# A Mamba-2 mixer on one core: x turned by VectorE through DRAM instead of by TensorE

## The chip, the core and the metric

The kernel runs on one core of one Trainium2 chip. The core has TensorE (PE in the profile; PEld is its weight load), VectorE (DVE), ScalarE (ACT), GpSimd (POOL) and SyncE (SP, which issues nearly all DMAs here). Each engine runs its own instructions in order and waits on semaphores for the others. The metric is the device time of the whole program in microseconds (us).

## The reference

A trunk of two layers on x of 2048 tokens by 1024 features, fp32. Layer 0 runs RG-LRU heads and latent attention side by side; layer 1 is a Mamba-2 mixer (SSD) with four groups. The change is in layer 1 alone:

```
proj = x @ w_in                                  # z 2048, xbc 3072, dt 32
xbc  = silu(conv4(xbc));  x, B, C = split(xbc)   # causal depthwise convolution, 4 taps
xf   = x * dt;  cs = cumsum(dt * a) over 128 tokens
decay[l,s] = exp(cs[l] - cs[s]) for s <= l
y    = (C B^T * decay) xf + exp(cs) * (C state)
state = state * exp(cs[-1]) + B^T (xf * exp(cs[-1] - cs))
y    = rmsnorm_per_group((y + d * x) * silu(z)) @ w_out
```

## The kernel before

Layer 1's projection and scan are one phase, `phase_ssd`, between some 1170 and 2350 us of the span. It has 16 **stages** n, four groups of heads g with four pieces c of 512 tokens in each. A stage computes ten projection **units** of 128 by 512: z0 to z3 (numbers 0 to 3), B (4), C (5) and x0 to x3 (6 to 9). Two units are worked as a pair. Full precision comes from three matmuls of high and low halves, so a pair takes 48 matmuls in four **ticks** of twelve; a stage has 20 ticks. The order of the units is the list that `unit_order` gives.

Everything else is laid between the matmuls by hand: `self.later(k, fn)` puts the instructions of `fn` into the program k ticks later. So the order on each engine is the order of the program, and nothing is rearranged at run time. After an x, B or C unit `conv` follows: ScalarE reads the unit out of PSUM (L1130), VectorE adds the three other taps (L1136), ScalarE applies SiLU (L1138).

While a stage projects, the four **steps** of the stage before are run, one for each 128 tokens, five ticks apart. A step has these parts, at ticks counted from its own start:

- `prep` at -4: SP loads the decays' tile e, 512 KB, from d_cs (L1216; L1124 loads a small table, `tab`, for j = 0). e has two buffers.
- `expo` at -1: ScalarE turns e into decays (L1223, L1224).
- `turn` at 0: x stands with features on partitions, and the scan wants tokens there. TensorE transposes the four 128x128 blocks into one PSUM bank px (L1231), transposes B (L1233) and forms C times B (L1234).
- `spread` at 0: VectorE reads px three times (L1242 t1, L1249 xf, L1256 xs), masks C B (L1246) and multiplies e by it (L1250).
- `split` at +2 (xd), `products` at +4 (TensorE L1273: e times xf; the old state) and `products2` with `state` at +5.
- `norm` at +6: ScalarE squares y and sums the squares (L1309). It needs some tile to write the squares to, and takes the first half of e.
- `scale` at +8, `back` at +10: VectorE turns y in 32x32 blocks into yo (L1319).
- `write` at +12: four SP stores of yo, 64 KB each, in pieces of 128 bytes, to d_y1 (L1325; the profile names it d_y).

The projected x1T is read through a ring of ten blocks of 512 KB (L1103): two loads in the middle of a stage, six in its last pair, each as a block comes free. Between two groups ten blocks of weights are loaded (L98) and split (L112, L129) by `load_at`, into slots that the units have finished with. After the last stage come four more steps, four ticks apart, and the output projection (L1401 to L1418), whose weights `out1_weights` loads over the last stage. A DMA on SP also has to wait until the eighth DMA before it has landed.

Of the kernel before, what the change touches and what calls it, by code (L numbers as in the profile page):

```python
# [14 lines left out]
P = 128  # L15
# [42 lines left out]
class K:  # L58
# [96 lines left out]
    def run(self):  # L155
        nc, tc, A = self.nc, self.tc, self.A
        with ExitStack() as ctx:
            dp = ctx.enter_context(tc.tile_pool(name="dram", bufs=1, space=bass.MemoryType.DRAM))
            core = ctx.enter_context(tc.tile_pool(name="core", bufs=1))
            ctx.enter_context(tc.manual_schedule())  # L160
            self.W = core.tile([P, 10, 2048], F32R, name="W")
            self.core = core
            self.stp = ctx.enter_context(tc.tile_pool(name="stp", bufs=2))
            self.ring = core.tile([P, 10, 1024], F32R, name="ring")
            self.cst = core.tile([P, NCST], F32, name="cst")
            self.im = core.tile([P, 2, 128], F32R, name="im")
            self.half = core.tile([P, 2], F32, name="half")
            nc.vector.memset(self.half[:, 0:1], -0.5)
            nc.vector.memset(self.half[:, 1:2], 0.5)
            self.ident = self.cst[:, C_ID:C_ID + 128]  # L170
            D = self.D = {}
            D["y0"] = dp.tile([NT, P, KB, P], F32, name="d_y0")
            D["sg"] = dp.tile([4, P, SEQ], F32, name="d_sg")
            D["kr"] = dp.tile([NCH, P, 2, 512], F32R, name="d_kr")
            D["q"] = dp.tile([8, NCH, P, 512], F32, name="d_q")
            D["k"] = dp.tile([4, NCH, P, 2, 512], F32R, name="d_k")
            D["x1"] = dp.tile([SEQ, DM], F32, name="d_x1")
            D["x1T"] = dp.tile([NCH, P, KB, 2, 512], F32R, name="d_x1T")
            D["li"] = dp.tile([len(GROUPS), 512], F32, name="d_li")
            D["cs"] = dp.tile([NT, 32, P], F32, name="d_cs")  # L180
            D["tab"] = dp.tile([NCH, 4, P, 4, 5, 8], F32, name="d_tab")

            D["y1"] = dp.tile([NT, 32, 4, 16, P], F32, name="d_y1")
            self.pp = ctx.enter_context(tc.tile_pool(name="ps", bufs=8, space=bass.MemoryType.PSUM))
            self.layer0()
            with ExitStack() as c2:
                self.l1c = c2.enter_context(tc.tile_pool(name="l1c", bufs=1))
                self.xst = self.l1c.tile([P, 2, 512], F32, name="xst")
                self.o0 = ExitStack()
                self.phase_out0(self.o0.enter_context(tc.tile_pool(name="o0", bufs=2)))  # L190
                with ExitStack() as c3:
                    self.phase_ssd(c3)
                    self.flush_of("phase_ssd")
            self.phase_out1()
            self.dump()
# [910 lines left out]
    def phase_ssd(self, ctx):  # L1106
# [16 lines left out]
            t = S[n]["tab"] = p.tile([P, 4, 5, 8], F32, tag="tab", name="tab", bufs=2)  # L1123
            nc.sync.dma_start(out=t, in_=D["tab"][c, g])  # L1124

        def conv(g, u, ps, o):

            b = blk(g, 6 + u if u < 4 else u)
            w = lambda k: vec[:, b, k:k + 1]
            nc.scalar.activation(out=o, in_=ps, func=AF.Identity, scale=w(3), bias=w(4))  # L1130

            def taps():
                for k in range(3):
                    d = 3 - k
                    for dst, src in ((o[:, d:], ps[:, :512 - d]), (o[:, :d], halo[:, u, k:])):
                        v.scalar_tensor_tensor(out=dst, in0=src, scalar=w(k), in1=dst, op0=ALU.mult, op1=ALU.add)  # L1136
                v.tensor_copy(halo[:, u], ps[:, 509:512])
                self.later(1, lambda: nc.scalar.activation(out=o, in_=o, func=AF.Silu))  # L1138
            self.later(1, taps)

        def terms(n, s):
            for kb in range(KB):
# [7 lines left out]
        def post(n, s, ps):  # L1150
            g, c = divmod(n, NCH)
            st = S[n]
            if s < 4:
                z = st["z", s] = p.tile([P, 512], F32, tag="z", name="z", bufs=6)
                nc.scalar.activation(out=z, in_=ps, func=AF.Silu)
            elif s >= 6:
                o = st["x", s - 6] = pc.tile([P, 512], F32, tag="xT", name="xT", bufs=7)
                conv(g, s - 6, ps, o)
            else:
                nm = "BC"[s - 4]  # L1160
                o = st[nm] = pc.tile([P, 512], F32, tag=nm, name=nm, bufs=2)
                conv(g, s, ps, o)
# [39 lines left out]
        def step(n, j, t0):  # L1202
# [16 lines left out]
            def expo():  # L1219
# [3 lines left out]
                    nc.scalar.activation(out=e[:, hd], in_=e[:, hd], func=AF.Relu, scale=-1.0, bias=cs[:, hd:hd + 1])  # L1223
                nc.scalar.activation(out=e, in_=e, func=AF.Exp, scale=-1.0)  # L1224

            def turn():

                st = S[n]
                px = R["px"] = self.psum()
                for u in range(4):  # L1230
                    nc.tensor.transpose(px[:, u * 128:u * 128 + 128], st["x", u][:, tok], self.ident)  # L1231
                pb = R["pb"] = self.psum()
                nc.tensor.transpose(pb[:, 0:128], st["B"][:, tok], self.ident)  # L1233
                nc.tensor.matmul(pb[:, 128:256], st["B"][:, tok], st["C"][:, tok], start=True, stop=True)  # L1234

            def spread():
                dt, cs, ecs, dd, cd = R["t"]
                px, pb = R["px"], R["pb"]
                xs = R["xs"] = p.tile([P, 512], F32, tag="xs", name="xs")
                if not last:  # L1240
                    t1 = R["t1"] = p.tile([P, 512], F32, tag="t1", name="t1")
# [63 lines left out]
            def norm():  # L1305
                y = R["y"]
                q = R["q"] = p.tile([P, 4], F32, tag="q", name="q", bufs=2)
                j2 = R["e"][:, 0:4].rearrange("p k n -> p (k n)")
                nc.scalar.activation(out=j2, in_=y, func=AF.Square, accum_out=q[:, 0:1])  # L1309
                nc.gpsimd.tensor_scalar(out=q[:, 1:2], in0=q[:, 0:1], scalar1=1.0 / 512, scalar2=1e-6, op0=ALU.mult, op1=ALU.add)  # L1310
                nc.gpsimd.tensor_tensor(out=q[:, 2:3], in0=q[:, 1:2], in1=self.half[:, 0:1], op=ALU.pow)

# [2 lines left out]

            def back():

                o = R["o"] = p.tile([P, 512], F32, tag="yo", name="yo", bufs=2)
                v.transpose(out=o, in_=R["y"])  # L1319

            def write():
                o = R["o"]
# [1 line left out]
                    r = slice(32 * b, 32 * b + 32)  # L1324
                    nc.sync.dma_start(out=D["y1"][tt, :, g, :, r], in_=o[r].rearrange("r (u s) -> r u s", s=32))  # L1325

            for at, fn in ((-4, prep), (-1, expo), (0, turn), (0, spread), (2, split), (4, products), (4, out), (5, products2), (5, state),
                           (6, norm), (8, scale), (10, back), (12, write)):
                self.later(t0 + at, fn)

# [9 lines left out]
        def unit_order(n):  # L1340
            if n == 0:
                return [4, 5, 6, 7, 8, 9, 0, 1, 2, 3]
            if n == N - 1:
                return [0, 1, 6, 7, 2, 8, 3, 4, 9, 5]
            return [4, 5, 6, 7, 8, 0, 1, 2, 3, 9] if n % NCH == 0 else [4, 5, 0, 6, 1, 7, 2, 8, 3, 9]

        for n in range(N):
            g, c = divmod(n, NCH)
# [2 lines left out]
                for j in range(4):  # L1351
                    step(n - 1, j, 5 + 5 * j)
            if c == NCH - 1 and g + 1 < 4:
                for s, at in ((4, 1), (5, 2), (6, 6), (7, 10), (8, 14), (0, 16), (1, 19), (2, 21), (3, 24), (9, 26)):
                    self.load_at(at, self.wslot(s), A["w1"][g + 1, s])
            if n == N - 1:
                self.out1_weights()
# [20 lines left out]
    def out1_weights(self):  # L1378
# [1 line left out]
        self.o1w = {}  # L1380
        self.nw = self.core.tile([P, 16], F32, name="nw")
        self.nc.sync.dma_start(out=self.nw, in_=self.A["nw"])
        for k, (sl, at) in enumerate(((4, 5), (5, 8), (6, 9), (0, 12), (1, 13), (2, 15), (3, 16), (8, 18), (9, 19), (7, 21))):
            self.o1w[k] = self.W[:, sl]
            self.load_at(at, sl, self.A["wo1"][k], rows=self.nw[:, 2 * (k % 8):2 * (k % 8) + 2])

# [226 lines left out]
```

## Time and profile before

| | us |
|---|---|
| median of 3 runs | 2650.51 (2649.64 to 2654.17) |
| profiled execution, whole | 2655.34 |
| its span, first to last instruction | 2653.2 |
| mean granted TensorE clock | 0.993 |
| DMA moved in the span | 334.24 MB |

The costliest groups of the mixer that the change touches, or that stand beside it (line, engine, operation, output and inputs, shapes, count, then busy us and mean ns of one, then the idle time of the engine ahead of them and what ended most of it):

```profile
L1223 ACT ACTIVATE e<-e,tab 128x128 f32<-128x128 f32 x512 | 156.5, 390 | 45.1 <-DMA e<-d_cs 45.1
L1136 DVE SCALAR_TENSOR_TENSOR xT<-ps,vec,xT 128x509 f32<-128x509 f32 (+2 forms) x192 | 143.2, 746 | 5.0
```

Durations of matmuls overlap, since they are pipelined; what one costs TensorE is read from the starts in the timeline.

### The profile page before, as it was taken

The page shows a single profiled execution, that of the slowest core. Times are in us where ns is not written, and L with a number is a line of the kernel's source. Part 1 is how long each engine was busy: PE and PEld are TensorE (multiplying, and loading weights), DVE is VectorE, ACT ScalarE, POOL GpSimd, SP SyncE. Part 2 cuts the span into 40 slices and gives each one's busy share as a digit, 9 for nine tenths or more (in the row PEclk, how much of TensorE's full clock was granted, in tenths as well). Part 3 has the DMA queues.
Part 4 walks back from the last instruction along what each step waited for, and adds up shares of the span by engine and source line. Part 5 has one row for each costly group of instructions (what it writes and reads, how often), then busy time and mean ns, then how long its engine had stood idle before and what let it go on. Part 6 is the DMA issues. An engine that isn't in the chain of part 4 may idle for free.

```text
span 2653.2 us, 40112 instructions
## 1 busy us (share of the span) xinstructions
PE 2584.2 (97%) x14248; PEld 2127.2 (80%) x14248; DVE 1798.5 (68%) x3341; ACT 1499.5 (57%) x3114; POOL 940.7 (35%) x884
## 2 busy tenths in 40 slices
PE   8999999999999999999999999999999999899998
PEld 6888887788888878788887888788877887778886
DVE  6777225888888867775668677776777667656532
ACT  5665335777777732234666766766667666532100
POOL 4446221132324544550334333432243232434321
PEclk9999999999999999999999999999999999899999
DMA  4223328221223346673345334534454434466420
GB/s 138 63 88 113 104 77 288 62 78 46 74 52 87 90 165 195 212 260 104 109 137 160 113 109 122 157 115 113 129 159 129 114 107 122 141 194 220 159 97 37
DMA packets 293991, 334.24 MB, mean 126 GB/s; under 512 B 151456, under 2 KB 209696, under 8 KB 293536
## 3 DMA queue, kind: packets, MB, share of 16 engines
q1 hardware_dynamic: 293792, 331.68, 40.7%
q8 instruction: 113, 1.85, 0.3%
q14 instruction: 86, 0.70, 0.1%
HBM read 245.82 MB, written 85.79 MB: 125 GB/s over the span
## 4 chain that ended last, share of the span: by engine, by line
PE 75%; DVE 11%; ACT 7%; issue 3%; DMA 3%; POOL 1%; SPq 0%; ACTq 0%; DVEq 0%; POOLq 0%
PE ps L1170 9%; PE ps L1172 9%; PE ps L1171 9%; PE ps L137 5%; PE ps L139 5%; PE ps L138 5%; PE ps L826 4%; PE ps L797 4%; PE ps L1416 4%; PE ps L1418 4%; PE ps L1417 4%; PE ps L932 2%; PE ps L1273 2%; PE ps L934 2%; PE ps L933 2%
## 5 line engine op out<-in xcount | busy, mean ns | idle before, releaser
L1170 PE MATMUL ps<-ring,W 128*128 128x512 f32 x768 | 305.5, 398 | 3.1 <-DMA ring<-d_x1T 2.9
L1172 PE MATMUL ps<-ring,W 128*128 128x512 f32 x768 | 300.0, 391 | 0.0
L1171 PE MATMUL ps<-ring,W 128*128 128x512 f32 x768 | 299.4, 390 | 0.0
L751 DVE TENSOR_REDUCE mx<-ps 128x1 f32<-128x512 f32 (+3 forms) x320 | 192.4, 606 | 55.8 <-PE ps L748 42.2
L1292 POOL TENSOR_TENSOR y<-y,xs 128x512 f32<-128x512 f32 x60 | 77.9, 1299 | 405.8 <-DVE y L1291 405.8
L767 ACT ACTIVATE pr<-ps,mx 128x512 f32<-128x512 f32 (+3 forms) x320 | 198.5, 629 | 16.9 <-DVE mx L755 14.6
L1170 PE MATMUL ps<-W,ring 128*128 128x512 f32 x512 | 201.2, 393 | 0.0
L1172 PE MATMUL ps<-W,ring 128*128 128x512 f32 x512 | 200.3, 391 | 0.0
L1171 PE MATMUL ps<-W,ring 128*128 128x512 f32 x512 | 199.9, 391 | 0.0
L797 PE MATMUL ps<-cst,pr 128*128 128x128 f32 x1088 | 174.8, 275 | 9.4 <-ACT pr L767 6.0
L1223 ACT ACTIVATE e<-e,tab 128x128 f32<-128x128 f32 x512 | 156.5, 390 | 45.1 <-DMA e<-d_cs 45.1
L1170 PEld LDWEIGHTS ps<-ring,W 128*128 128x128 f32 x768 | 144.4, 188 | 36.3 <-DMA ring<-d_x1T 7.5
L1172 PEld LDWEIGHTS ps<-ring,W 128*128 128x128 f32 x768 | 144.2, 188 | 31.0
L1171 PEld LDWEIGHTS ps<-ring,W 128*128 128x128 f32 x768 | 144.4, 188 | 28.5
L129 DVE TENSOR_TENSOR W<-ps,W 128x512 fp32r<-128x512 f32 (+3 forms) x261 | 144.6, 560 | 28.5 <-ACT W L614 18.3
L797 PEld LDWEIGHTS ps<-cst,pr 128*128 128x128 f32 x1088 | 129.4, 141 | 42.9 <-ACT pr L767 10.7
L1138 ACT ACT_TABLE_LOAD x58 | 74.4, 1283 | 148.8 <-DVE xT L1136 79.2
L1401 ACT CAST ring<-ring 128x1024 fp32r<-128x1024 f32 x50 | 51.6, 1048 | 185.0 <-PE ps L1417 132.0
L129 POOL TENSOR_TENSOR ring<-ring 128x1024 fp32r<-128x1024 f32 (+1 forms) x41 | 84.8, 2067 | 190.0 <-ACT ring L1401 174.1
L129 POOL TENSOR_TENSOR W<-st,W 128x512 fp32r<-128x512 f32 (+2 forms) x70 | 111.6, 1601 | 107.6 <-ACT W L112 93.3
L1136 DVE SCALAR_TENSOR_TENSOR xT<-ps,vec,xT 128x509 f32<-128x509 f32 (+2 forms) x192 | 143.2, 746 | 5.0
L803 ACT CAST W<-ps 128x512 fp32r<-128x512 f32 (+2 forms) x213 | 110.8, 526 | 55.3 <-PE ps L797 53.6
(347 smaller groups left out, 7449.7 us busy)
## 6 DMA issues: line engine op xcount, KB each, us to landing
ring<-d_x1T SPq DMA_DIRECT2D x128, 512.0 KB
e<-d_cs SPq DMA_DIRECT2D x64, 512.0 KB
ring<-d_y SPq DMA_DIRECT2D x100, 256.0 KB
st<-in_w_dram SPq DMA_DIRECT2D x40, 512.0 KB
d_x1T<-xt SPq DMA_DIRECT2D x32, 512.0 KB
d_y<-yo SPq DMA_DIRECT2D x256, 64.0 KB
st<-in_wo_dram SPq DMA_DIRECT2D x24, 512.0 KB
xs<-in_xT_dram SPq DMA_DIRECT2D x23, 512.0 KB
```

The costliest lines, as they stand in the source:

```text
L129: eng.tensor_tensor(out=out, in0=src, in1=hi.bitcast(F32), op=ALU.subtract)
L137: self.nc.tensor.matmul(ps, ah, bh, start=(i == 0), stop=False)
L138: self.nc.tensor.matmul(ps, ah, bl, start=False, stop=False)
L139: self.nc.tensor.matmul(ps, al, bh, start=False, stop=(i == n - 1))
L751: v.tensor_reduce(out=m[:, kc:kc + 1], in_=ps[:, 0:nw], axis=AX.X, op=ALU.max, negate=True)
L767: nc.scalar.activation(out=prob[n][:, o:o + nw], in_=ps[:, 0:nw], func=AF.Exp, bias=nm, accum_out=acc)
L797: nc.tensor.transpose(ps[:, i * 128:i * 128 + 128], prob[n][:, o:o + 128], self.ident)
L1136: v.scalar_tensor_tensor(out=dst, in0=src, scalar=w(k), in1=dst, op0=ALU.mult, op1=ALU.add)
L1170: nc.tensor.matmul(ps, ah, bh, start=(k == 0), stop=False)
L1171: nc.tensor.matmul(ps, ah, bl, start=False, stop=False)
L1172: nc.tensor.matmul(ps, al, bh, start=False, stop=(k == KB - 1))
L1223: nc.scalar.activation(out=e[:, hd], in_=e[:, hd], func=AF.Relu, scale=-1.0, bias=cs[:, hd:hd + 1])
```

## The change

x is turned once per projected unit by VectorE instead of once per step by TensorE. After SiLU a new part, `turn_x`, transposes the unit in 32x32 blocks into a tile xo. A tick later SP stores it to a new DRAM tile d_xt in four stores of 64 KB, which place the blocks so that token rows come out. Each step then loads its 128 tokens of x, 256 KB, into a tile xk (`load`, three ticks ahead of the step, one tick for j = 0), and `spread` reads xk where it read px. The four transposes and their PSUM bank are gone, and xT needs three buffers instead of seven.

Apart from that, `norm` writes its squares into yo, which it now takes four ticks earlier than `back` did, so e is no longer touched after `products`. The order of the units is changed so that x0 and x1 come first and C last in most stages, and the weight slots are loaded in a matching order.

```diff
--- before.py
+++ after.py
@@ -179,6 +179,8 @@
             D["li"] = dp.tile([len(GROUPS), 512], F32, name="d_li")
             D["cs"] = dp.tile([NT, 32, P], F32, name="d_cs")
             D["tab"] = dp.tile([NCH, 4, P, 4, 5, 8], F32, name="d_tab")
+
+            D["xt"] = dp.tile([4 * NCH, 16, 32, 512], F32, name="d_xt")
 
             D["y1"] = dp.tile([NT, 32, 4, 16, P], F32, name="d_y1")
             self.pp = ctx.enter_context(tc.tile_pool(name="ps", bufs=8, space=bass.MemoryType.PSUM))
@@ -1123,7 +1125,7 @@
             t = S[n]["tab"] = p.tile([P, 4, 5, 8], F32, tag="tab", name="tab", bufs=2)
             nc.sync.dma_start(out=t, in_=D["tab"][c, g])
 
-        def conv(g, u, ps, o):
+        def conv(g, u, ps, o, after=None):
 
             b = blk(g, 6 + u if u < 4 else u)
             w = lambda k: vec[:, b, k:k + 1]
@@ -1135,8 +1137,25 @@
                     for dst, src in ((o[:, d:], ps[:, :512 - d]), (o[:, :d], halo[:, u, k:])):
                         v.scalar_tensor_tensor(out=dst, in0=src, scalar=w(k), in1=dst, op0=ALU.mult, op1=ALU.add)
                 v.tensor_copy(halo[:, u], ps[:, 509:512])
-                self.later(1, lambda: nc.scalar.activation(out=o, in_=o, func=AF.Silu))
+                self.later(1, silu)
+
+            def silu():
+                nc.scalar.activation(out=o, in_=o, func=AF.Silu)
+                if after:
+                    self.later(1, after)
             self.later(1, taps)
+
+        def turn_x(n, u, o):
+
+            xo = pc.tile([P, 512], F32, tag="xo", name="xo", bufs=2)
+            v.transpose(out=xo, in_=o)
+
+            def store():
+                for a in range(4):
+                    k, r = 128 * u + 32 * a, slice(32 * a, 32 * a + 32)
+                    nc.sync.dma_start(out=D["xt"][n, :, :, k:k + 32].rearrange("b i j -> i b j"),
+                                      in_=xo[r].rearrange("i (b j) -> i b j", j=32))
+            self.later(1, store)
 
         def terms(n, s):
             for kb in range(KB):
@@ -1154,8 +1173,8 @@
                 z = st["z", s] = p.tile([P, 512], F32, tag="z", name="z", bufs=6)
                 nc.scalar.activation(out=z, in_=ps, func=AF.Silu)
             elif s >= 6:
-                o = st["x", s - 6] = pc.tile([P, 512], F32, tag="xT", name="xT", bufs=7)
-                conv(g, s - 6, ps, o)
+                o = pc.tile([P, 512], F32, tag="xT", name="xT", bufs=3)
+                conv(g, s - 6, ps, o, lambda: turn_x(n, s - 6, o))
             else:
                 nm = "BC"[s - 4]
                 o = st[nm] = pc.tile([P, 512], F32, tag=nm, name=nm, bufs=2)
@@ -1223,19 +1242,19 @@
                     nc.scalar.activation(out=e[:, hd], in_=e[:, hd], func=AF.Relu, scale=-1.0, bias=cs[:, hd:hd + 1])
                 nc.scalar.activation(out=e, in_=e, func=AF.Exp, scale=-1.0)
 
+            def load():
+                x = R["x"] = p.tile([P, 512], F32, tag="xk", name="xk", bufs=2)
+                nc.sync.dma_start(out=x, in_=D["xt"][n, 4 * j:4 * j + 4].rearrange("b i j -> (b i) j"))
+
             def turn():
-
                 st = S[n]
-                px = R["px"] = self.psum()
-                for u in range(4):
-                    nc.tensor.transpose(px[:, u * 128:u * 128 + 128], st["x", u][:, tok], self.ident)
                 pb = R["pb"] = self.psum()
                 nc.tensor.transpose(pb[:, 0:128], st["B"][:, tok], self.ident)
                 nc.tensor.matmul(pb[:, 128:256], st["B"][:, tok], st["C"][:, tok], start=True, stop=True)
 
             def spread():
                 dt, cs, ecs, dd, cd = R["t"]
-                px, pb = R["px"], R["pb"]
+                px, pb = R["x"], R["pb"]
                 xs = R["xs"] = p.tile([P, 512], F32, tag="xs", name="xs")
                 if not last:
                     t1 = R["t1"] = p.tile([P, 512], F32, tag="t1", name="t1")
@@ -1305,8 +1324,9 @@
             def norm():
                 y = R["y"]
                 q = R["q"] = p.tile([P, 4], F32, tag="q", name="q", bufs=2)
-                j2 = R["e"][:, 0:4].rearrange("p k n -> p (k n)")
-                nc.scalar.activation(out=j2, in_=y, func=AF.Square, accum_out=q[:, 0:1])
+
+                o = R["o"] = p.tile([P, 512], F32, tag="yo", name="yo", bufs=2)
+                nc.scalar.activation(out=o, in_=y, func=AF.Square, accum_out=q[:, 0:1])
                 nc.gpsimd.tensor_scalar(out=q[:, 1:2], in0=q[:, 0:1], scalar1=1.0 / 512, scalar2=1e-6, op0=ALU.mult, op1=ALU.add)
                 nc.gpsimd.tensor_tensor(out=q[:, 2:3], in0=q[:, 1:2], in1=self.half[:, 0:1], op=ALU.pow)
 
@@ -1315,8 +1335,7 @@
 
             def back():
 
-                o = R["o"] = p.tile([P, 512], F32, tag="yo", name="yo", bufs=2)
-                v.transpose(out=o, in_=R["y"])
+                v.transpose(out=R["o"], in_=R["y"])
 
             def write():
                 o = R["o"]
@@ -1324,7 +1343,7 @@
                     r = slice(32 * b, 32 * b + 32)
                     nc.sync.dma_start(out=D["y1"][tt, :, g, :, r], in_=o[r].rearrange("r (u s) -> r u s", s=32))
 
-            for at, fn in ((-4, prep), (-1, expo), (0, turn), (0, spread), (2, split), (4, products), (4, out), (5, products2), (5, state),
+            for at, fn in ((-4, prep), (-3 if j else -1, load), (-1, expo), (0, turn), (0, spread), (2, split), (4, products), (4, out), (5, products2), (5, state),
                            (6, norm), (8, scale), (10, back), (12, write)):
                 self.later(t0 + at, fn)
 
@@ -1341,8 +1360,8 @@
             if n == 0:
                 return [4, 5, 6, 7, 8, 9, 0, 1, 2, 3]
             if n == N - 1:
-                return [0, 1, 6, 7, 2, 8, 3, 4, 9, 5]
-            return [4, 5, 6, 7, 8, 0, 1, 2, 3, 9] if n % NCH == 0 else [4, 5, 0, 6, 1, 7, 2, 8, 3, 9]
+                return [0, 1, 6, 7, 2, 8, 3, 9, 4, 5]
+            return [6, 7, 4, 8, 9, 0, 1, 2, 3, 5] if n % NCH == 0 else [6, 7, 0, 4, 1, 8, 2, 9, 3, 5]
 
         for n in range(N):
             g, c = divmod(n, NCH)
@@ -1351,7 +1370,7 @@
                 for j in range(4):
                     step(n - 1, j, 5 + 5 * j)
             if c == NCH - 1 and g + 1 < 4:
-                for s, at in ((4, 1), (5, 2), (6, 6), (7, 10), (8, 14), (0, 16), (1, 19), (2, 21), (3, 24), (9, 26)):
+                for s, at in ((6, 1), (7, 2), (4, 6), (8, 10), (9, 14), (0, 16), (1, 19), (2, 21), (3, 24), (5, 26)):
                     self.load_at(at, self.wslot(s), A["w1"][g + 1, s])
             if n == N - 1:
                 self.out1_weights()
@@ -1380,7 +1399,7 @@
         self.o1w = {}
         self.nw = self.core.tile([P, 16], F32, name="nw")
         self.nc.sync.dma_start(out=self.nw, in_=self.A["nw"])
-        for k, (sl, at) in enumerate(((4, 5), (5, 8), (6, 9), (0, 12), (1, 13), (2, 15), (3, 16), (8, 18), (9, 19), (7, 21))):
+        for k, (sl, at) in enumerate(((4, 5), (5, 8), (6, 9), (0, 12), (1, 13), (2, 15), (3, 16), (7, 18), (8, 19), (9, 21))):
             self.o1w[k] = self.W[:, sl]
             self.load_at(at, sl, self.A["wo1"][k], rows=self.nw[:, 2 * (k % 8):2 * (k % 8) + 2])
```

On PE, at one step in a regular stage, there stood behind the three matmuls of the state update (L137 to L139):

```order
5136 L137 MATMUL ps<-xd,bh 128x512
5137 L138 MATMUL ps<-xd,bh 128x512
5138 L139 MATMUL ps<-xd,bh 128x512
5139 L1231 MATMUL ps<-cst,xT 128x128 x4
5140 L1233 MATMUL ps<-cst,B 128x128
5141 L1234 MATMUL ps<-C,B 128x128
5142 L1170 MATMUL ps<-W,ring 128x512
```

and in the changed program at the same place (L1252 and L1253 are the old L1233 and L1234, L1189 the old L1170):

```order
5131 L137 MATMUL ps<-xd,bh 128x512
5132 L138 MATMUL ps<-xd,bh 128x512
5133 L139 MATMUL ps<-xd,bh 128x512
5134 L1252 MATMUL ps<-cst,B 128x128
5135 L1253 MATMUL ps<-C,B 128x128
5136 L1189 MATMUL ps<-W,ring 128x512
```

The four transposes of x are gone; the transpose of B and the product with C are left.

On SP, from the load of e for step 3 to that of the next stage's step 0, the queue was this (e is the decays' tile, ring the projection's input, d_y_82 the stores of y):

```order
442 L1216 DMA e<-d_cs 128x1024
443 L1103 DMA ring<-d_x1T 128x1024 x2
444 L1325 DMA d_y_82<-yo 32x16x32 x4
445 L1103 DMA ring<-d_x1T 128x1024 x4
446 L1124 DMA tab<-d_tab 128x160
447 L1216 DMA e<-d_cs 128x1024
448 L1325 DMA d_y_82<-yo 32x16x32 x4
```

and is now (L1235 is the load of e, L1344 the stores of y, L1247 the new loads of x, L1156 its new stores):

```order
486 L1235 DMA e<-d_cs 128x1024
487 L1105 DMA ring<-d_x1T 128x1024 x2
488 L1344 DMA d_y_83<-yo 32x16x32 x4
489 L1247 DMA xk<-d_xt 128x512
490 L1156 DMA d_xt<-xo 32x16x32 x4
491 L1105 DMA ring<-d_x1T 128x1024 x4
492 L1156 DMA d_xt<-xo 32x16x32 x4
493 L1126 DMA tab<-d_tab 128x160
494 L1235 DMA e<-d_cs 128x1024
495 L1344 DMA d_y_83<-yo 32x16x32 x4
```

Four stores of x2 have come ahead of the last four ring loads, and four of x3 ahead of the table and of the e of step 0.

On VectorE, in `spread` of a step in a regular stage, the operations are now:

```order
1798 L1261 TENSOR_TENSOR t_13041<-xk,tab 128x512
1799 L1265 TENSOR_TENSOR cbm<-ps,cst 128x128
1800 L129 TENSOR_TENSOR bh<-ps,bh 128x128
1801 L1268 TENSOR_TENSOR xf<-xk,tab 128x512
1802 L1269 TENSOR_TENSOR e<-e,cbm 128x1024
1803 L1275 TENSOR_TENSOR xs<-xk,dsk 128x512
1804 L1151 STREAM_TRANSPOSE xo<-xT 128x512
1805 L129 TENSOR_TENSOR xd<-t_13041,xd 128x512
```

Three of them read xk in SBUF where they read the PSUM bank (they were L1242, L1249 and L1256), and the turn of an x block, L1151, stands between them and xd, the input of the state update. This is so at two of a stage's four turns; the other two stand elsewhere.

## The prediction

> **What bounds the kernel now.** I read the page's busy times first, then its chain that ended last, then the stretches of the mixer one by one, because a share over the whole span hides that the mixer has three kinds of stretch.
>
> ```profile
> span 2653.2 us, 40112 instructions
> PE 2584.2 (97%) x14248; PEld 2127.2 (80%) x14248; DVE 1798.5 (68%) x3341; ACT 1499.5 (57%) x3114; POOL 940.7 (35%) x884
> PE 75%; DVE 11%; ACT 7%; issue 3%; DMA 3%; POOL 1%; SPq 0%; ACTq 0%; DVEq 0%; POOLq 0%
> ```
>
> TensorE (PE) is busy 97% of the span and is 75% of the chain. But 11% of the chain is VectorE (DVE) and 7% ScalarE (ACT), so somewhere the others set the end. The mixer's time can be cut into stretches (columns: window, its length, then busy us and count for PE, PEld, DVE, ACT, POOL, then the granted clock, DMA share, GB/s):
>
> ```profile
> 1240.00:1325.00 85.00, 85.00 (x524) 69.78 (x524) 57.78 (x113) 55.02 (x109) 24.03 (x29) 1.00 0.29 86
> 1411.00:1500.00 89.00, 87.12 (x527) 69.86 (x526) 70.68 (x128) 65.80 (x125) 38.54 (x40) 1.00 0.51 155
> 1700.00:1789.00 89.00, 86.61 (x529) 69.85 (x528) 64.61 (x117) 63.15 (x118) 34.77 (x36) 1.00 0.49 150
> 1976.00:2065.00 89.00, 86.52 (x526) 69.48 (x525) 65.05 (x117) 64.08 (x122) 33.97 (x35) 1.00 0.50 152
> 2230.00:2300.00 70.00, 60.52 (x356) 48.16 (x357) 56.59 (x86) 50.17 (x95) 26.04 (x21) 0.91 0.49 144
> ```
>
> In a **regular** stretch (first row) PE has no gap at all: 85.00 of 85.00. Around each of the three **boundaries** between weight groups (next three rows) PE is idle 1.88, 2.39 and 2.48 us, VectorE is at 73 to 79%, and the chain there passes through weight conversion, ScalarE's decays and VectorE. In the **tail** (last row) PE is idle 9.48 of 70 us and VectorE busy for 81%. A shorter PE program pays in full only in the first kind.
>
> **The transposes that go.** The PE timeline of one step and of the next:
>
> ```profile
> 1304.06 0.60 PE L1231 MATMUL ps<-cst,xT 128*128 128x128 f32 x4
> 1304.49 0.27 PE L1233 MATMUL ps<-cst,B 128*128 128x128 f32 x1
> ...
> 1321.18 0.60 PE L1231 MATMUL ps<-cst,xT 128*128 128x128 f32 x4
> ```
>
> The four transposes of L1231 start at 1304.06 and the next matmul at 1304.49: they hold PE for 0.43 us of a step of 1321.18 - 1304.06 = 17.12 us. In 64 steps that is 64 x 0.43 = 27.5 us, the most that this part can give.
>
> ```profile
> L1231 PE MATMUL ps<-cst,xT x256: 270/272/421, 1236.3 to 2329.4; 128*128 128x128 f32 x128
> ```
>
> Each lasts 272 ns, which would make 256 x 0.272 = 69.6 us. But the starts are 0.109 us apart (0.43 / 4): matmuls overlap, and the pitch is what a removed one gives back. I take the pitch. The Trainium skill ("TensorE: Matmul & The Clock Gate", Part 4: PE-mode transpose) gives some 275 ns for a 128x128 transpose inside a kernel; the duration agrees, and by that figure as a cost the gain would be 70 us, but the starts of this trace speak for 27.5.
>
> My count of where PE sets the end: each boundary reaches over about 8 steps (ten weight blocks converted over 26 ticks, five to a step, and some three steps in which the others catch up), the tail over the last 7. So 64 - 3 x 8 - 7 = 33 steps are free: **33 x 0.43 = -14.2 us**.
>
> **The turn on VectorE.** The same operation on the same tile shape stands in the trace, with the stores that follow it:
>
> ```profile
> L1319 DVE STREAM_TRANSPOSE yo<-y x64: 681/704/712, 1271.7 to 2356.7; 128x512 f32<-128x512 f32 x64
> L1325 SPq DMA_DIRECT2D d_y<-yo x256: 318/530/2438, 1278.0 to 2359.5; - x128
> ```
>
> 64 more transposes of 0.70 us are 45 us of VectorE. In the regular stretch it idles 85.00 - 57.78 = 27.2 us in five steps, and five turns are 3.5 us: hidden, though two of the four turns of a stage stand ahead of the product xd that PE's state update reads. If that cover were gone, each would cost up to 0.70. In a boundary five of the turns fall on a VectorE that has 18 to 24 us left of 89 and passes work back and forth with ScalarE.
>
> **x from SBUF instead of PSUM.** Three operations per step change their source; their cost from the nearest rows:
>
> ```profile
> L1249 DVE TENSOR_TENSOR xf<-ps,tab 128x512 f32<-128x512 f32 x64 | 43.4, 678 | 0.0
> L1250 DVE TENSOR_TENSOR e<-e,cbm x64: 1207/1215/2358, 1238.7 to 2340.6; 128x1024 f32<-128x1024 f32 x64
> L1250 DVE TENSOR_TENSOR e<-e,cbm 128x1024 f32<-128x1024 f32 x64 | 95.3, 1489 | 0.0
> ```
>
> From PSUM one takes 678 ns. L1250 reads SBUF alone: at its median 1215 ns for twice the width, so 0.61 for this one, 0.07 less. But its mean is 1489, up to 2358, so it is sometimes held up, by 1489 / 1215 = 1.23 on average; that applied to 0.678 is +0.16. Three per step: from -0.2 to +0.47 us. I take +0.1, the middle of the two; in the regular stretch it is hidden, in boundary and tail it is 0.1 per step. The Trainium skill ("SBUF — State Buffer", SBUF: two separate sides) has a rule against this edit: a VectorE operation with two SBUF inputs and a GpSimd operation that reads SBUF share a port pair under an exclusive lock, and the second waits the whole instruction. The spread of L1250 agrees; by the rule the sum goes towards the upper end, +0.47.
>
> The PSUM bank that comes free ends the only PSUM wait of PE in the mixer:
>
> ```profile
> PE ps L1233 <- DVE y L1290: 3.0, 3, 1.0
> ```
>
> Three waits of 1.0 us, which I put one to a boundary: -1.0 each.
>
> **DMA and SP.** New per stage: four times four 64 KB stores and four loads of 256 KB. SP's queue now, at the end of one stage and the start of the next:
>
> ```profile
> 1324.27 2.15 SPq L1325 DMA_DIRECT2D d_y<-yo  x4
> 1345.21 0.34 SPq L1216 DMA_DIRECT2D e<-d_cs  x1
> 1345.95 0.81 SPq L1103 DMA_DIRECT2D ring<-d_x1T  x2
> 1346.87 5.12 SPq L1325 DMA_DIRECT2D d_y<-yo  x4
> 1352.09 4.60 SPq L1103 DMA_DIRECT2D ring<-d_x1T  x4
> 1356.78 0.38 SPq L1124 DMA_DIRECT2D tab<-d_tab  x1
> 1358.04 0.32 SPq L1216 DMA_DIRECT2D e<-d_cs  x1
> ```
>
> Four stores hold SP for 2.15 us, and 5.12 where it has to wait for earlier transfers. The store of block x3 comes in front of the table, the decays e of step 0 and whatever follows; its own wait is for VectorE's turn. So e(0) comes 2.15 to 5.12 us later, in every stage that follows one whose x3 is in the fourth pair (all but the first of each group). For the other three steps the second edit helps: the load of e no longer waits for the Square.
>
> ```profile
> SPq L1216 <- ACT e L1309: 434.4, 59, 16.1
> SPq L1216 <- PE ps L1273: 191.2, 40, 9.3
> ```
>
> ```profile
> ACT e L1223 <- DMA e<-d_cs: 45.1, 19, 4.4
> ...
> PE ps L1273 <- DVE e L1250: 5.1, 2, 3.7
> ...
> PE ps L1170 <- DMA ring<-d_x1T: 2.9, 8, 0.9
> ```
>
> SP stood 434.4 us behind that Square, 59 times, and ScalarE 45.1 us for e; but PE waited for the masked e only twice, 5.1 us in all. So in regular steps e has slack both ways and I put both edits at **nothing**; the cover is that slack, and without it each late e(0) costs up to 5.12. With the Square gone the load of e waits for PE's products, which read the tile before it (191.2 us already), so it moves up by a few us, not to the front. The ring loads also come earlier with it; PE lost 2.9 us to them. Bandwidth: a stage moves 8 x 512 KB of ring blocks, 4 x 512 KB of e and 16 x 64 KB of y, 7 MB; x out and back adds 2 MB, so the DMA share of 0.29 in a regular stretch would become some 0.37, and 0.51 at a boundary some 0.6: room, as long as SP issues in time.
>
> **Boundary, net.** The freed PE is 8 x 0.43 = 3.4 us. Against it 5 turns x 0.70 = 3.5, 8 x 0.1 = 0.8 and a late e(0), 1.1 (half the lower end): 5.4 us of VectorE and ScalarE. PE is idle only 2.4 of 89 us there, so the end passes from one to the other; I take half of each, -1.7 + 2.7, and half of the PSUM wait, -0.5: +0.5. Ends: -3.4 - 2.4 = -5.8 and +5.4. Three boundaries: **+1.5** (from -17 to +16).
>
> **Tail, net.** Here the chain does stop for e:
>
> ```profile
> 2297.79 2.44 ACT L1223 ACTIVATE e<-e,tab 128x128 f32<-128x128 f32 x8 [3.86 <-DMA e<-d_cs]
> ...
> 2315.49 2.45 ACT L1223 ACTIVATE e<-e,tab 128x128 f32<-128x128 f32 x8 [3.73 <-DMA e<-d_cs]
> ```
>
> Two waits of 3.86 and 3.73 us for loads that the Square held back: -7.6. Against it two turns, 1.4, seven times 0.1, 0.7, and e(0) late by up to 5.1: +7.2. Net **-0.4** (from -10 to +7).
>
> **Sum.** -14.2 + 1.5 - 0.4 = -13.1 us. The profiled execution took 2655.34 us (span 2653.2), so it would become 2642.2. The median of the runs shown is 2650.51, 4.8 below that execution; with the same difference I predict **2637**.
>
> **The rivals.**
>
> *PE sets the end everywhere* (chance 0.25). All 64 steps give 0.43, and part of the 6.75 us of boundary idling goes with the ring, PSUM and e waits: -27.5 to -34, so 2616 to 2623. For it: PE is 75% of the chain and idles under 3% at a boundary. Against: DVE and ACT are 18% of the chain, and that is where the turns are added.
>
> *e(0) late in regular stages too* (0.17). The x3 store waits for a turn behind VectorE's work, and SP issues in order, so table, e(0) and the y stores wait behind it. If step 0 loses 1 us of PE in each of the 15 stages that hold steps of another, 15 us are gone and with the sum of the forecast the time is 2652. For it: 5.12 us in the row above. Against: only two PE waits for e in 64 steps.
>
> *VectorE becomes the bound* (0.16, slower). In 31 boundary and tail steps the turn (0.70) and the dearer reads (0.47) add 1.17 us each to the engine that sets the end: 36 us, if all of it is on the chain; less the free 14.2 that is +22, 2672. It gives a slower kernel once over 40% of it, 14.2 us, is on the chain; with two thirds, 24 - 14.2 = +10: **2660**. For it: VectorE at 81% in the tail. Against: over a quarter of the boundary it is idle.
>
> *A transpose costs its duration* (0.02): -69.6, 2581; the pitch is against it.
>
> **How the numbers follow.** The forecast has the remaining 0.40, with 2632 to 2645 as its own range. Runs of this kernel differ by about 0.2%, 5 us, which is what a measurement can tell from no change. Faster by more: the forecast almost whole, the first and the last rival, 0.66. Within: the e(0) rival and a rest of the forecast, 0.18. Slower: the third rival, 0.16. The range takes in the first rival and the unchanged time, 2617 to 2655, and leaves out most of the slower rival and a sliver below.
>
> **What would show it.** Right: regular steps of 16.69 us instead of 17.12 and PE without gaps there; 128 VectorE transposes of 0.70; SP no longer behind the Square; boundary PE idle at 2 to 6 us per 89. Wrong: PE waits for e(0) or for xd in regular stretches (then the second rival); L1249's successor at 0.8 us and VectorE over 85% at boundaries (the third); PE idle gone at the boundaries (the first).

## The result

| | us | ratio to before, 95% interval |
|---|---|---|
| before, median of 4 runs | 2652.34 (2649.64 to 2655.68) | |
| changed, median of 4 runs | 2698.1 (2693.67 to 2703.76) | 1.0174 [1.0162, 1.0186] |
| profiled execution of the changed kernel, whole / span | 2700.12 / 2698.3 | |

The change makes the kernel 46 us slower. The page after, busy times and chain:

```profile
PE 2581.3 (96%) x13992; PEld 2110.3 (78%) x13992; DVE 1889.4 (70%) x3405; ACT 1502.1 (56%) x3114; POOL 972.2 (36%) x884
PE 55%; DVE 21%; ACT 9%; DMA 6%; issue 5%; SPq 3%; POOL 1%; ACTq 0%; DVEq 0%; POOLq 0%
```

PE's share of the chain has fallen from 75 to 55%; VectorE's has gone from 11 to 21%, and SP's queue, which was at 0, has 3%. The same stretches (window, its length, busy us and count of PE, PEld, DVE, ACT, POOL, then granted clock, DMA share, GB/s):

```profile
1240.00:1325.00 85.00, 85.00 (x513) 69.37 (x512) 64.29 (x118) 51.83 (x103) 23.05 (x25) 1.00 0.44 114
1411.00:1500.00 89.00, 83.05 (x465) 66.87 (x464) 75.94 (x128) 66.31 (x124) 41.58 (x37) 0.97 0.52 143
1700.00:1789.00 89.00, 82.75 (x462) 65.47 (x460) 76.24 (x128) 66.26 (x125) 41.57 (x37) 0.98 0.54 142
1976.00:2065.00 89.00, 82.33 (x483) 65.56 (x482) 76.08 (x127) 58.09 (x108) 39.34 (x36) 0.96 0.59 162
```

The regular stretch is still without a gap in PE. At the boundaries PE idles 6 to 7 us of 89 where it idled about 2, and VectorE is at 85%. The clock granted to PE is 0.96 to 0.98 there, where it was 1.00; that is 2 to 4 us of each 89 if PE set the pace throughout (an estimate from these rows), and no run separates it. Where the time went is read from the starts of B's transpose, which comes once per step. In the timeline of PE, two steps of a regular stage, then the first three of the eight steps at a boundary and the first step behind them:

```profile
1288.33 0.27 PE L1252 MATMUL ps<-cst,B 128*128 128x128 f32 x1
1305.02 0.27 PE L1252 MATMUL ps<-cst,B 128*128 128x128 f32 x1
...
1373.00 0.27 PE L1252 MATMUL ps<-cst,B 128*128 128x128 f32 x1
1394.10 0.27 PE L1252 MATMUL ps<-cst,B 128*128 128x128 f32 x1
1414.38 0.27 PE L1252 MATMUL ps<-cst,B 128*128 128x128 f32 x1
...
1528.85 0.27 PE L1252 MATMUL ps<-cst,B 128*128 128x128 f32 x1
```

A regular step takes 1305.02 - 1288.33 = 16.69 us, 0.43 less than before. Boundary steps take 21.1 and 20.3. The two stages of a boundary take 1528.85 - 1373.00 = 155.9 us; before the same eight steps ran from 1372.97 to 1512.64:

```profile
1372.97 0.27 PE L1233 MATMUL ps<-cst,B 128*128 128x128 f32 x1
1512.64 0.27 PE L1233 MATMUL ps<-cst,B 128*128 128x128 f32 x1
```

That is 139.7, so 16.2 us more at this boundary. The same sums for all stretches, from these starts in each trace (regular: the eight stages away from boundaries; tail: the seven steps from the start of the last stage but one's steps):

| kernel | regular, 32 steps | three boundaries, 24 steps | tail |
|---|---|---|---|
| before | 545.0 | 419.7 | 128.1 |
| changed | 533.9 | 463.7 | 135.7 |
| difference | -11.1 | +44.0 | +7.6 |

These make +40.5 of the 45.1 us between the spans. What holds a boundary up stands in the chain of the changed kernel at its beginning (start, us, what):

```profile
1361.76 1.98 DVE e L1269
1363.74 0.60 DVE xs L1275
1364.34 0.63 DVE xo L1151
1364.99 0.32 SPq L1156
...
1367.05 0.46 SPq L1126
1367.50 0.05 issue
1367.61 4.74 DMA e<-d_cs
1372.39 0.04 issue
1372.44 1.65 ACT e L1242 x6
1374.09 4.72 DMA e<-d_cs
```

VectorE does the whole spread of step 3, then the turn of x3 (xo L1151). Only then can SP issue the store of x3, then the table (L1126), then e of step 0, which lands 4.74 us later, and e of step 1 6.5 us behind it. In SP's timeline the hole is plain:

```profile
1353.20 1.88 SPq L1105 DMA_DIRECT2D ring<-d_x1T  x4
1364.99 1.96 SPq L1156 DMA_DIRECT2D d_xt<-xo  x4
1367.05 0.46 SPq L1126 DMA_DIRECT2D tab<-d_tab  x1
1367.61 0.38 SPq L1235 DMA_DIRECT2D e<-d_cs  x1
```

From 1355.1 to 1365.0 SP issues nothing. Before, e of step 0 went out at 1358.04, now at 1367.61.

That is the beginning of a boundary. Its last step is long as well, 1528.85 - 1506.58 = 22.3 us, and what PE waits for between these two starts is not e but the ring (line that waits, what it waits for, us, times, longest):

```profile
PE ps L1189 <- DMA ring<-d_x1T: 3.3, 5, 1.4
```

In the second stage of a boundary x3 is projected in the third pair, so its store stands ahead of the ring loads. SP's timeline:

```profile
1490.99 0.43 SPq L1235 DMA_DIRECT2D e<-d_cs  x1
1502.36 3.13 SPq L1156 DMA_DIRECT2D d_xt<-xo  x4
1505.59 0.92 SPq L1105 DMA_DIRECT2D ring<-d_x1T  x2
...
1511.04 2.16 SPq L1105 DMA_DIRECT2D ring<-d_x1T  x4
```

Again SP issues nothing for 11 us, and the ring blocks come too late. In that step the clock granted to PE falls as well, to 0.67 between 1512 and 1516. Of SP's waits the largest is now this one (line that waits, engine and line waited for, us, times, longest):

```profile
SPq L1156 <- DVE xo L1151: 314.3, 39, 19.7
```

In the regular stages the same wait costs little: all but three of the 32 steps are as short as the missing transposes make them. Whether it, VectorE's added work or another part of the change costs the 44 us at the boundaries is what the runs had to tell.

### The profile page after: what moved, and what is told of

Its sections match the earlier page's. It is cut to its first block, busy times and chain, and to the rows that moved or that the text cites. A ratio compares the mean times of both kernels' runs of the same rounds, so it can differ in the third digit from the quotient of the medians.

```text
span 2698.3 us, 40162 instructions
## 1 busy us (share of the span) xinstructions
PE 2581.3 (96%) x13992; PEld 2110.3 (78%) x13992; DVE 1889.4 (70%) x3405; ACT 1502.1 (56%) x3114; POOL 972.2 (36%) x884
## 4 chain that ended last, share of the span: by engine, by line
PE 55%; DVE 21%; ACT 9%; DMA 6%; issue 5%; SPq 3%; POOL 1%; ACTq 0%; DVEq 0%; POOLq 0%
PE ps L137 4%; PE ps L138 4%; PE ps L139 4%; PE ps L828 4%; PE ps L799 4%; PE ps L1189 4%; PE ps L1191 4%; PE ps L1190 4%; PE ps L1435 3%; PE ps L1437 3%; PE ps L1436 3%; DVE xT L1138 3%; DVE e L1269 2%; DMA ring<-d_x1T 2%; PE ps L934 2%
## 5 line engine op out<-in xcount | busy, mean ns | idle before, releaser
L1189 PE MATMUL ps<-ring,W 128*128 128x512 f32 x768 | 309.5, 403 | 11.8 <-DMA ring<-d_x1T 11.7
L1189 PE MATMUL ps<-W,ring 128*128 128x512 f32 x512 | 203.4, 397 | 0.0
L1189 PEld LDWEIGHTS ps<-ring,W 128*128 128x128 f32 x768 | 146.0, 190 | 49.4 <-DMA ring<-d_x1T 20.6
L1242 ACT ACTIVATE e<-e,tab 128x128 f32<-128x128 f32 x512 | 156.5, 390 | 44.1 <-DMA e<-d_cs 44.0
```

The costliest lines, as they stand in the source:

```text
L1189: nc.tensor.matmul(ps, ah, bh, start=(k == 0), stop=False)
```

## The experiments

The theories: **V**, VectorE is overloaded by the turns and the slower reads of x; **Q**, the stores of x wait in SP's order and hold the loads behind them; **O**, the new order of units; **S**, the squares in yo. Each run's ratio is to runs of the kernel before on the same chip. The runs come from three chips, on which the kernel before has medians of 2652.49, 2650.99 and 2651.40 us, so a difference between runs of two chips is good to 1 or 2 us.

**Squares alone.** The kernel before, with

```diff
-                j2 = R["e"][:, 0:4].rearrange("p k n -> p (k n)")
-                nc.scalar.activation(out=j2, in_=y, func=AF.Square, accum_out=q[:, 0:1])
+                o = R["o"] = p.tile([P, 512], F32, tag="yo", name="yo", bufs=2)
+                nc.scalar.activation(out=o, in_=y, func=AF.Square, accum_out=q[:, 0:1])
```

and `back` writing to the same yo.

> The kernel before with one part of the change: the squares go to yo instead of e. V (VectorE is what the change overloads: the turn and the slower reads of x from SBUF): this part is harmless, the tail's two waits for e go, 2643 to 2651. Q (SP's order is what costs: the stores of x wait for the turn and hold the loads behind them): the same, 2643 to 2651. S (the squares now wait for the stores of y out of yo, and that holds ScalarE): slower than before by 10 us or more, 2660 and up, with ScalarE waits for d_y at the boundaries.

Measured: 2643.14 us, ratio 0.9962 [0.9947, 0.9977]. S falls; this part of the change gains 9 us by itself. Its boundaries take 414.2 us, its tail 126.1. ScalarE's waits for e go from 45.1 us to this:

```profile
ACT e L1223 <- DMA e<-d_cs: 8.6, 4, 4.1
```

**Order alone.** The kernel before with the new lists of units and weight slots, and

```diff
-                o = st["x", s - 6] = pc.tile([P, 512], F32, tag="xT", name="xT", bufs=7)
+                o = st["x", s - 6] = pc.tile([P, 512], F32, tag="xT", name="xT", bufs=8)
```

> The kernel before with one part of the change: the new order of units and of the weight slots (x0 and x1 first, C last), xT with 8 buffers. V and Q: within 5 us of before, since neither the work of VectorE nor SP's queue changes. O (the order is what costs: C last, or the weight blocks in the other order, come too late at the boundaries): slower by 20 us or more, 2670 to 2700, in the same two stages per boundary as the changed kernel.

Measured: 2652.48 us, ratio 0.9998 [0.9989, 1.0008]. O falls.

**No turn.** The changed kernel with

```diff
-            xo = pc.tile([P, 512], F32, tag="xo", name="xo", bufs=2)
-            v.transpose(out=xo, in_=o)
+            xo = o
```

> The changed kernel without VectorE's turn of x: the stores take xT as it is, so x is not turned and the output is not the reference's; all DMAs, loads and SBUF reads stay. V: most of the loss goes, since 44 us of VectorE go: 2645 to 2665, VectorE at 80% or less in the boundary windows. Q: the stores still wait in SP's order, now for SiLU, one step earlier: about half the loss stays, 2665 to 2685. O: no change, 2690 to 2700.

Measured: 2658.8 us, ratio 1.0023 [1.0013, 1.0033]: 39 of the 46 us are gone. It is V's range, and by itself it speaks for V, but the stores then wait for SiLU instead of the turn, so it also takes away most of what Q blames: SP's waits ahead of the stores go from 314.3 to 184.4 us, and the first and the last step of each boundary are as short as with late stores.

**Late stores.** The changed kernel with

```diff
-            xo = pc.tile([P, 512], F32, tag="xo", name="xo", bufs=2)
+            xo = pc.tile([P, 512], F32, tag="xo", name="xo", bufs=3)
-            self.later(1, store)
+            self.later(3, store)
```

> The changed kernel with the stores of x three ticks behind the turn instead of one (xo with 3 buffers), so that SP hardly waits for VectorE and the table and e of step 0 go ahead of the stores of x3. Q: most of the loss goes, 2640 to 2665. V: little changes, 2685 to 2705, with the boundaries as long as before. O: no change, 2690 to 2700.

Measured: 2659.14 us, ratio 1.0024 [1.0015, 1.0034]. All turns are still there, and the same 39 us are gone: Q. The expectation of V, no change, is missed by 26 us or more.

**No turn and late stores.** Both edits, xT with 4 buffers.

> The changed kernel with the stores of x three ticks later and without VectorE's turn: the stores take xT as it is (4 buffers), so x is not turned and the output is not the reference's. V (what the late stores left, 16 us over the kernel with the squares in yo alone, is VectorE's work at the boundaries): 44 us of turns less there and in the tail, 2630 to 2645. Q (it is still SP's queue and the DMA traffic): 2652 to 2660.

Measured: 2651.92 us, ratio 1.0006 [0.9997, 1.0015], 6 to 7 us below the late stores alone. So once SP's order is mended, VectorE's 44 us of turns are worth 6 to 7, found at the boundaries (429.0 against 434.8 us) and in the tail (132.4 against 135.4). Neither range holds it; Q's misses it by 0.1 us.

**The turn beside the old path.** The kernel before with squares in yo, the turns into a scratch tile and late stores of xT; PE's transposes, the PSUM reads and the old order stay, nothing loads d_xt:

```diff
+            xo = p.tile([P, 512], F32, tag="xo", name="xo")
+            v.transpose(out=xo, in_=o)
...
-            self.later(1, store)
+            self.later(3, store)
```

> The kernel before with the squares in yo, and with VectorE's turns of x and late stores in addition (not in the first stage); the turn's result goes to a scratch tile, the stores write xT, nothing loads them. TensorE's transposes, the PSUM reads and the order of units are those of before. It does the reference's work and the turn's beside it. V with the slower SBUF reads as the larger part: the turns alone cost little, 2645 to 2655. V with the turns as the larger part: 2655 to 2670, boundary steps of 18.5 to 20 us. Q: SP's stores alone cost, 2655 or more, with SP waiting and VectorE under 80% at boundaries.

Measured: 2652.87 us, ratio 1.0005 [0.9995, 1.0014], some 10 us above the squares alone. That is V's first range: turns and stores together cost some 10, so they are not the larger part. Boundaries take 420.0 us, against 414.2 with the squares alone and 434.8 with late stores and the whole new path.

**xs on GpSimd.** The kernel with late stores and

```diff
-                v.tensor_tensor(out=bc(xs), in0=bc(px), in1=hb(dsk[:, 8 * g:8 * g + 8]), op=ALU.mult)
+                nc.gpsimd.tensor_tensor(out=bc(xs), in0=bc(px), in1=hb(dsk[:, 8 * g:8 * g + 8]), op=ALU.mult)
```

> The changed kernel with the stores of x three ticks later, and the skip term xs = d x computed by GpSimd from xk instead of by VectorE (0.79 us of VectorE per step less). V: boundaries and tail gain about 0.5 us a step in 31 steps, 2635 to 2650. Lock (the two engines stand in each other's way in SBUF, so GpSimd's work comes back as slower VectorE reads): 2655 to 2670.

Measured: 2650.16 us, ratio 0.9995 [0.9985, 1.0005], some 8 us below the late stores and 0.2 above V's range; that of Lock, 2655 to 2670, is missed.

**Squares back in e.** The changed kernel with the old `norm`, undoing the squares' part alone.

> The changed kernel with the squares back in e. If the squares in yo help as they did alone (9 us): 2703 to 2712. If in the changed kernel they hurt, since yo's stores land late behind the stores of x and ScalarE waits for them (4 waits, 19.8 us in its trace): 2675 to 2692. Within 4 us of the changed kernel: neither.

Measured: 2718.69 us, ratio 1.0253 [1.0238, 1.0268]. In the changed kernel the squares in yo save 20 us, twice what they save alone. None of the three ranges holds it. The load of e waits for the Square again, in a queue that already waits for turns (SP's waits):

```profile
SPq L1235 <- ACT e L1329: 322.7, 45, 17.2
SPq L1156 <- DVE xo L1151: 180.5, 33, 20.5
```

Together that is 503 us of SP for these two, against 314 for the second alone in the changed kernel.

**Which store.** The changed kernel with `self.later(3 if u == 3 else 1, store)`, then with `3 if u < 3 else 1` (xo with 3 buffers in both).

> The changed kernel with only the stores of x3 three ticks behind the turn (xo with 3 buffers); those of x0 to x2 one tick behind it, as in the change. Q3 (what holds SP up is the store of x3, which stands ahead of the table and of e for steps 0 and 1): most of the 39 us come back, 2658 to 2670. Q012 (it is the stores of x0 to x2, which hold e of steps 2 and 3, the ring and the weight blocks): 2685 to 2700.

> The other half: only the stores of x0 to x2 three ticks behind the turn, x3 one tick as in the change. Q3: 2685 to 2700. Q012: 2658 to 2670. If both halves give about half, 2675 to 2685 each, every store that waits costs alike.

Measured: 2659.79 us, ratio 1.0032 [1.0022, 1.0042], for x3 late; 2698.75, ratio 1.0175 [1.016, 1.019], for the other three late: both in the ranges of Q3. The whole 39 us hang on one store in four, that of x3. SP's timeline at the same boundary, with x3 late:

```profile
1350.19 0.40 SPq L1126 DMA_DIRECT2D tab<-d_tab  x1
1350.69 0.49 SPq L1235 DMA_DIRECT2D e<-d_cs  x1
...
1356.67 2.77 SPq L98 DMA_DIRECT2D st<-in_w_dram  x1
1359.64 2.19 SPq L1156 DMA_DIRECT2D d_xt<-xo  x4
```

and with the other three late:

```profile
1351.64 14.69 SPq L1156 DMA_DIRECT2D d_xt<-xo  x8
1366.43 0.46 SPq L1126 DMA_DIRECT2D tab<-d_tab  x1
1366.99 0.37 SPq L1235 DMA_DIRECT2D e<-d_cs  x1
```

e of step 0 goes out at 1350.69 or at 1366.99, though the edit moves no work of any engine. With x3 late the boundary runs from 1368.89 to 1513.85 (the starts of B's transpose): 145.0 us, 10.9 less than in the changed kernel: 4.4 in the first step, behind e of step 0, and 6.3 in the last, behind the ring loads. Over the three boundaries 28.8 us come back, 13.0 in the first steps and 14.3 in the last ones. So about half of what x3's store costs at the boundaries goes by way of e and half by way of the ring.

**Squares and order.** The kernel before with both edits.

> The kernel before with the squares in yo and the new order of units (xT with 8 buffers), TensorE's transposes and PSUM reads kept. If the order is neutral here too: 2640 to 2647. If C last costs once e comes early (SiLU of C and B holds ScalarE ahead of xd, as in the 20.2 us step of the late-store kernels): 2650 to 2660.

Measured: 2644.57 us, ratio 0.9969 [0.9957, 0.9982]. The order is neutral here too.

**xs on GpSimd, later.** The kernel with late stores, with xs in a part `skip` at tick +3 instead of in `spread`:

```diff
+            def skip():
+                nc.gpsimd.tensor_tensor(out=bc(R["xs"]), in0=bc(R["x"]), in1=hb(dsk[:, 8 * g:8 * g + 8]), op=ALU.mult)
```

> The changed kernel with all stores three ticks behind the turn and xs computed by GpSimd three ticks into the step, when VectorE's spread is over. Lock (VectorE and GpSimd hold each other up when both read SBUF at once): t1, xf and e are undisturbed by xs, better than the 2650 of xs at once: 2638 to 2648. V alone: the same, 2647 to 2653. If GpSimd comes too late for y: over 2655.

Measured: 2641.18 us, ratio 0.9956 [0.9941, 0.9971]: faster than the kernel before and level with the squares alone (2643.14; the two intervals overlap). It is in the range of Lock, 9 us below xs in `spread`: the same work on the same engines a few us apart. The second place also changes what stands behind xs on GpSimd. The step's `xf` on VectorE, first with xs at once, then three ticks later:

```profile
L1268 DVE TENSOR_TENSOR xf<-xk,tab 128x512 f32<-128x512 f32 x64 | 74.0, 1156 | 0.0
```

```profile
L1268 DVE TENSOR_TENSOR xf<-xk,tab 128x512 f32<-128x512 f32 x64 | 49.2, 768 | 0.0
```

The masked e behind it went the other way, from 1354 to 1621 ns, so xf and e together are down by 8 us over the 64 steps, not by the 25 of xf alone. Its stretches: regular 531.3 us, boundaries 422.8, tail 128.7.

## Why the prediction was wrong

- **The free PE time was right.** Predicted 33 steps x 0.43 = -14.2. With SP's order mended the 32 regular steps take 531.3 instead of 545.0 us, -13.7, and a step takes 16.69, the number given. In the change as it is it was -11.1: three of the 32 steps are longer, 17.9, 16.9 and 17.8 us, in two of them with PE waiting 0.7 and 0.5 us for xd. With x3's store late all three are short.
- **The step that failed: "e(0) late" as a term of 1.1 us per boundary, and of 5.1 in the tail.** The forecast took +1.5 us for the three boundaries and -0.4 for the tail; they came out at +44.0 and +7.6. The prediction saw that x3's store comes ahead of the table and e and that its own wait is for VectorE's turn, but then sized the delay by the 2.15 to 5.12 us that four stores take to issue. The wait itself was left out. The turn stands behind `spread` in VectorE's program, and that engine runs late there, so SP stood for 10 us (1355.1 to 1365.0) before the first store. e(0) came 9.6 us later, and e(1) behind it. The same wait holds the ring loads at the end of a boundary, for which the sum has no term, since they were expected to come earlier. x3 late and x3 early differ by 39 us: some 10 per boundary (463.7 against 434.9 over three), half of it behind e(0) and half behind the ring, 3 in the tail, 3 in regular steps.
- **The rival "e(0) late in regular stages too" had the mechanism and the wrong place.** Regular steps had the slack that the prediction said; the boundaries, where ScalarE and VectorE set the end, had little. The rival "VectorE becomes the bound" gave the sign, and its mark, VectorE over 85% at the boundaries, was just reached; but 39 of the 46 us go with all turns still on VectorE, so the larger part is another mechanism.
- **The squares' gain was put in the wrong place.** The prediction gave them 7.6 us in the tail and nothing elsewhere. Alone they gain 9.4 us (2652.49 to 2643.14), of which the tail has 2.0 (128.1 to 126.1) and the boundaries, where no gain was put down for an earlier e, 5.5 (419.7 to 414.2).
- **The boundaries, VectorE's part.** With SP's order mended the boundaries take 434.8 us, against 414.2 with the squares alone: +6.9 for each, where the prediction had bounds of -5.8 to +5.4 and took +0.5. Of the eight steps of the first boundary three became 0.4 us shorter, as PE's part should, and five 0.6 to 3.1 us longer. The turns are the smaller part: 1.9 us per boundary, both when they are taken away (434.8 to 429.0) and when they are added to the squares alone (414.2 to 420.0). That leaves 5 us per boundary, which go by elimination with the reads of x from SBUF and its loads; no run changes the reads alone.
- **x from SBUF.** Predicted -0.2 to +0.47 us per step, taken +0.1. The three operations in the changed kernel:

```profile
L1261 DVE TENSOR_TENSOR t<-xk,tab 128x512 f32<-128x512 f32 x60 | 61.9, 1031 | 19.3 <-DMA e<-d_cs 19.3
L1275 DVE TENSOR_TENSOR xs<-xk,dsk 128x512 f32<-128x512 f32 x64 | 50.7, 793 | 0.0
L1268 DVE TENSOR_TENSOR xf<-xk,tab 128x512 f32<-128x512 f32 x64 | 49.1, 767 | 10.6 <-DMA xk<-d_xt 10.6
```

They were 683, 679 and 678 ns, so +0.35, +0.11 and +0.09, together +0.55 per step, above the upper end. In the timelines of the two engines, in a regular step of the kernel with late stores, the first of them overlaps GpSimd's split of C, for 0.4 us:

```profile
1318.50 0.95 DVE L1261 TENSOR_TENSOR t<-xk,tab 128x512 f32<-128x512 f32 x1
```

```profile
1318.30 0.60 POOL L129 TENSOR_TENSOR ch<-C,ch 128x128 fp32r<-128x128 f32 x1 [2.10 <-ACT ch L1273]
```

It takes 0.95 us instead of 0.68. In the kernel before, reading PSUM, it overlapped the same split and took 0.68:

```profile
1306.31 0.68 DVE L1242 TENSOR_TENSOR t<-ps,tab 128x512 f32<-128x512 f32 x1
```

```profile
1306.11 0.60 POOL L129 TENSOR_TENSOR ch<-C,ch 128x128 fp32r<-128x128 f32 x1 [1.17 <-ACT ch L1254]
```

In each of the two traces this overlap, 0.4 us on average, occurs in 54 of the 60 steps; the median of the 54 is 683 ns with x in PSUM and 953 with x in SBUF. On GpSimd, xs beside xf or apart from it changes xf from 1156 to 768 ns. The Trainium skill ("SBUF — State Buffer", SBUF: two separate sides) has these two engines share ports under an exclusive lock when VectorE has two SBUF inputs and GpSimd reads SBUF. These rows agree with it, 0.27 us longer for an overlap of 0.4.

What stays open: how much of the boundaries' last 20 us (434.8 less 414.2) is VectorE's own time and how much the collision with GpSimd. Moving xs off VectorE and away from `spread` wins 12 us of it back (422.8), but does both at once; and the 9 us between the two places of xs are in part the collision's and may in part be the new order on GpSimd.

## What to carry to other kernels

A DMA that waits for a late engine costs what is queued behind it on its issuing engine, whichever load that is: size it by how long that engine lags there, read from its timeline, not by the time to issue, and place it behind the loads that others wait for. Where a stretch is set by a chain over two other engines, time taken off the third is worth little there, and time added to the two can cost more than it wins elsewhere; sum such stretches separately, step by step. Take a change of several parts apart: here one part alone gained 9 us, one was neutral, and the third lost 39 by a single position in a queue and 16 more beside it (late stores against the squares alone).

## What the runs showed that was not expected

An fp32 VectorE product reading SBUF instead of PSUM is no faster where nothing disturbs it: xf's median is 677 ns against 678. A single 128x512 product of VectorE went up to 2895 ns (xs in the changed kernel, median 680) while GpSimd was splitting a block of `ring`:

```profile
L1275 DVE TENSOR_TENSOR xs<-xk,dsk x64: 676/680/2895, 1241.9 to 2382.6; 128x512 f32<-128x512 f32 x64
L1268 DVE TENSOR_TENSOR xf<-xk,tab x64: 674/677/1386, 1240.2 to 2379.3; 128x512 f32<-128x512 f32 x64
```

In the timelines of VectorE and GpSimd the longest one and the split beside it are

```profile
2303.08 2.90 DVE L1275 TENSOR_TENSOR xs<-xk,dsk 128x512 f32<-128x512 f32 x1
```

```profile
2302.44 2.99 POOL L129 TENSOR_TENSOR ring<-ring 128x1024 fp32r<-128x1024 f32 x1 [1.96 <-ACT ring L1420]
```

The two overlap for 2.35 us, from 2303.08 to 2305.43, and xs takes 2.2 us more than its median: it stood for nearly all of the overlap.
